# The planner's table of durations and landings revised in a list-scheduled two-layer mixer block

## The chip, the cores and the metric

The kernel runs on one core of a Trainium2 chip. The metric is device time of one execution in microseconds (us), the median of several runs of the same program. One further execution is recorded by the hardware profiler; its rows are what is read below.

## What is computed

The reference is a block of two layers (`DEPTH = 2`) for 256 latent tokens and 256 context tokens of width 1024, all in float32. Cut to what matters:

```python
for l in range(DEPTH):
    need_ctx = l < DEPTH - 1
    hl = xl * (1.0 + sc1) + sh1                      # sc, sh, g: from w_ada[l] and the conditioning vector
    hc = xc * (1.0 + xsc1) + xsh1
    out_l, out_c = token_mixers(hl, hc, ...)         # one input projection, 4 mixers, gated sum, out projection
    xl = layer_norm(ALPHA * xl + g1 * out_l, ...)
    hl = xl * (1.0 + sc2) + sh2
    xl = layer_norm(ALPHA * xl + g2 * swiglu(hl, w_gate_up[l], w_down[l]), ...)
    if need_ctx:
        ...                                          # the same for the context tokens
return xl
```

The four mixers are multi-head latent attention (MLA), neighbourhood attention, differential attention and grouped-query attention (GQA). Each one's output goes through a projection of its own, is multiplied by a sigmoid gate, and the four are summed. In the second layer the context tokens are only keys and values, so its later parts work on 256 columns where the first layer's work on 512.

## The kernel before, in words

**Tiles.** Tokens lie along the free dimension: `hh` and `hl` hold the modulated input of all 512 tokens, eight tiles of 128 channels. A float32 product is made of three passes on TensorE (`mm3`): every operand `x` is split into a rounded part `hi` and a rest `lo`, and hi·hi, hi·lo and lo·hi are accumulated. A weight of 128 x 1024 (512 KB) is loaded by SyncE's queue into `wr`, ScalarE casts it to `wh`, VectorE subtracts to get `wl`; each of the three has a ring of three buffers (`load_w`). So a weight is a chain load, cast, subtract, and then its matmuls `mm<-wh,hh`, `mm<-wl,hh`, `mm<-wh,hl`.

**Stages.** For each layer: adaLN vectors (in the first layer by strips of 32 columns, `st<-wr,cc`, later by VectorE reductions `raw<-wr,silbc`), input projection, the four mixers, gates (`gt`), branch products (`mm<-y,wh`, `mm<-y,wl`), out projection, layer norm, the FFN with 22 tiles of 128, layer norm. Some steps move data between partitions by DMA from SBUF to SBUF (`q<-raw`, `k<-q`, `l<-q`, `k<-k`). GpSimd does the small powers: `rk`, `rq`, `rms`, `rg`, `lnr` to the exponent -0.5 (`mhalf`).

**What sets the order.** The program is not written in the order in which it runs. All operations are first recorded in a `Plan` (11034 of them); `price` gives each a cost in us, and `schedule` makes ten list schedules (`PASSES = 10`). `forward` simulates the five engines, the rotating buffers, and one DMA queue, and at each step takes the ready operation of the highest priority on the engine that can start first. `backward` simulates from the end and sets the priorities for the next pass. The forward order of the smallest modelled length is kept, and `emit` writes each engine's operations in it, one phase after the other. Nothing of the model runs on the chip: there each engine takes its instructions in the order written and waits on semaphores. All instructions therefore carry the line number of the emitting line (L540; strips L538), and the rows are told apart by tile names.

The names that matter: `Op`'s slots (L205), `price` (L281), `backward` (L331; DMA at L367 to L370), `forward` (L381; DMA at L479 to L483).

Of the kernel before, what the change touches and what calls it, by code (L numbers as in the profile page):

```python
# [11 lines left out]
F32R = mybir.dt.float32r  # L12
# [191 lines left out]

class Op:  # L205
    __slots__ = ("eng", "meth", "args", "kw", "phase", "idx", "preds", "succs", "npred", "tiles", "cost",
                 "prio", "prio2", "rest", "nafter", "start", "end", "est", "nrot", "bytes", "dge", "ins", "lab")


class _Eng:  # L210
# [21 lines left out]
class Plan:  # L232
# [47 lines left out]
    def price(self, op, ins, outs):  # L280

        eng, kw = op.eng, op.kw
        if eng == "tensor":
            if op.meth == "matmuls":
                return sum(k["rhs"].free() for k in kw["each"]) / 2400 / 4 * (1 if kw["each"][0]["rhs"].dtype == F32R else 4) + 0.1
            if op.meth == "transpose":
                n = kw["in_"].shape[0]
                return max(64, n) * 2.1 / 2400
            n = max(64, kw["rhs"].free())
            return n / 2400 + 0.0026 if kw["rhs"].dtype == F32R else n * 4 / 2400 + 0.43  # L290
        n = max([v.free() for v in outs + ins] or [1])
        ps_in = any(v.tile.pool.psum for v in ins)
        ps = ps_in or any(v.tile.pool.psum for v in outs)
        if eng == "scalar":
            ptr = sum(1 for k in ("bias", "scale") if isinstance(kw.get(k), View)) + ("accum_out" in kw)
            return (0.05 if ps_in else 0.09) + n * 0.833e-3 + 0.093 * ptr
        if eng == "vector":
            if op.meth == "reciprocal":
                return 0.065 + n * 8 / 960
            ptr = sum(1 for k in ("scalar", "scalar1", "scalar2") if isinstance(kw.get(k), View))  # L300
            if op.meth == "tensor_scalar" or op.meth == "tensor_copy":
                return 0.065 + 0.06 * ptr + n / 960 / (1 if ps else 2)
            return 0.065 + 0.065 * ptr + n / 960
        if eng == "gpsimd":
            if kw.get("op") == ALU.pow:
                return 0.3 + n * 0.17
            return 0.16 + n * 2.2e-3
        op_bytes = 1
        for v in (outs or ins):
            op_bytes = v.shape[0] * v.free() * 4  # L310
        op.bytes = op_bytes
        op.dge = 0.65 if outs and ins else 0.46
        return 0.05

    def schedule(self):
# [19 lines left out]
    def backward(self, order):  # L335

        ready = {e: [] for e in self.ENGINES}
        free = {e: 0.0 for e in self.ENGINES}
        heirs = {}
        for op in order:  # L340
            after = set(op.succs)
            for t in op.tiles:
                if t.next is not None:
                    after |= t.next.users
            op.nafter, op.rest = len(after), 0.0
            heirs[op] = after
        before = {op: [] for op in order}
        for op in order:
            for s in heirs[op]:
                before[s].append(op)  # L350
            if op.nafter == 0:
                ready[op.eng].append(op)
            for t in op.tiles:
                t.turn = 0.0
        dma, done = 0.0, 0
        while done < len(order):
            best = None
            for e in self.ENGINES:
                if ready[e]:
                    t = max(free[e], min(o.rest for o in ready[e]))  # L360
                    if best is None or t < best[0]:
                        best = t, e
            t, e = best
            op = max((o for o in ready[e] if o.rest <= t + LOOK_BACK), key=lambda o: (o.end, o.idx))
            ready[e].remove(op)
            t = max(t, op.rest)
            if e == "sync":  # L367
                dma = max(dma, t + 0.95) + max(op.bytes / 360e3, op.dge)
                free[e] = dma - 0.95
                op.prio2 = dma + 1.1  # L370
            else:
                free[e] = op.prio2 = t + op.cost
            done += 1
            for p in before[op]:
                p.rest = max(p.rest, op.prio2 + SEE[p.eng].get(e, SEE_OTHER[p.eng]))
                p.nafter -= 1
                if p.nafter == 0:
                    ready[p.eng].append(p)
        for op in order:
            op.prio = -op.prio2  # L380
            for t in op.tiles:  # L381
                t.turn = min(t.turn, op.prio)

    def forward(self):
# [13 lines left out]
        def grant(tile, slot):  # L398
            if slot.last is not None:
                slot.last.next = tile  # L400
            tile.slot, slot.last = slot, tile
            for w in tile.waiters:
                w.est = max(w.est, slot.ready)
                w.nrot -= 1
                if w.npred == 0 and w.nrot == 0:
                    push(w)

        queue, slots, first = {}, [], []
        for ph, pools in enumerate(self.phases):
            at, new = 0, []  # L410
            for p in pools:
                for tag, row in p.tags.items():
                    size = -(-max(t.row for t in row) * 4 // 32) * 32
                    row = sorted((t for t in row if t.left), key=lambda t: t.turn)
                    n = min(len(row), row[0].bufs if row else 0)
# [17 lines left out]
        free = {e: 0.0 for e in self.ENGINES}  # L433
# [8 lines left out]
        def advance(e):  # L442
            while cur[e] < nph and nleft.get((e, cur[e]), 0) == 0:
                cur[e] += 1
                for o in held[e].pop(cur[e], []):
                    ready[e].append(o)

        def push(op):
            if op.phase > cur[op.eng]:
                held[op.eng].setdefault(op.phase, []).append(op)  # L450
            else:
                ready[op.eng].append(op)
# [8 lines left out]
        dge_free, dma_free, done, order = 0.0, 0.0, 0, []  # L461
        while done < len(ops):
            best = None
            for e in self.ENGINES:
                if not ready[e]:
                    continue
                t = max(free[e], min(o.est for o in ready[e]))
                if best is None or t < best[0]:
                    best = (t, e)
            if best is None:  # L470
                return None
            t, e = best
            lim = t + LOOK[e]
            op = min((o for o in ready[e] if o.est <= lim), key=lambda o: (o.prio, o.idx))
            ready[e].remove(op)
            op.start = max(t, op.est)
            free[e] = op.start + op.cost
            op.end = free[e]
            if e == "sync":  # L479
                dge_free = max(op.end, dge_free) + op.dge  # L480
                dma_free = max(dge_free + 0.65, dma_free) + op.bytes / 360e3
                op.end = dma_free + 0.95
                free[e] = max(free[e], dma_free - 2.5)  # L483
            see = op.end + SEE_OTHER[e]
            order.append(op)
            done += 1
            nleft[(e, op.phase)] -= 1
            for s in op.succs:
                s.est = max(s.est, op.end + SEE[e].get(s.eng, SEE_OTHER[e]))
                s.npred -= 1  # L490
                if s.npred == 0 and s.nrot == 0:
                    push(s)
            for tl in op.tiles:
                if tl.pool.psum:

                    for o in tl.users:
                        if o.eng != e:
                            o.est = max(o.est, op.end + SEE[e].get(o.eng, SEE_OTHER[e]))
                tl.left -= 1
                slot = tl.slot  # L500
                slot.ready = max(slot.ready, see)
                if tl.left == 0:
                    q = queue[(tl.pool, tl.tag)]
                    if q:
                        grant(q.pop(), slot)
                        continue
                    for new, t in slot.after:
                        new.ready = max(new.ready, slot.ready)
                        new.wait -= 1
                        if new.wait == 0:  # L510
                            grant(t, new)
            advance(e)
# [1312 lines left out]
```

## Time and profile before

| | us |
|---|---|
| median of 3 runs | 1368.88 |
| lowest, highest | 1368.81, 1370.12 |
| profiled execution | 1369.86 |
| its span, first to last instruction | 1367.9 |
| TensorE busy | 1347.7 |
| VectorE busy | 989.7 |
| ScalarE busy | 643.1 |
| GpSimd busy | 65.4 |

The profiled execution lies 0.98 us above the median, and 1.96 us of it lie outside the span. A matmul's busy time overlaps with the next one's, and its end is modelled, so TensorE's busy share says only that it rarely stood idle. How often it did is in the rows of its waits, and in the starts of neighbouring rows of its timeline: in a timeline row the first number is the start, the second the length of the row, and a bracket names the idle time ahead of it and what ended that. The mean granted clock of TensorE is 0.998 of full speed.

### The profile page before, as it was taken

What the parts mean: (1) busy time and instruction counts of PE and PEld (TensorE: products, weight loads), DVE (VectorE), ACT (ScalarE), POOL (GpSimd) and SP (SyncE); (2) the same over time, 40 slices, a digit from 0 to 9 for tenths busy, and PEclk for the clock granted to TensorE, in tenths of its full rate; (3) what the DMA queues carried; (4) which work ended last, traced back from release to release, by engine and by line L of the source; (5) the groups of instructions that cost most, each with busy time, mean ns of one, the idle gap of its engine ahead of it and who ended that gap; (6) DMA issues with size and microseconds to landing.
All of it is one profiled execution on the core that took longest, in us unless ns stands there. A gap on an engine that the chain in (4) does not pass through costs nothing.

```text
span 1367.9 us, 20685 instructions
## 1 busy us (share of the span) xinstructions
PE 1347.7 (99%) x7804; PEld 1171.5 (86%) x7804; DVE 989.7 (72%) x1753; ACT 643.1 (47%) x1160; POOL 65.4 (5%) x124
## 2 busy tenths in 40 slices
PE   7999999999999999999999999999999999999997
PEld 4789889888878889888888888899999899899986
DVE  3697899997875778777655463868979878855554
ACT  3576676633754422223222121467857566544430
POOL 0000100122000000000000000101000200000000
PEclk9999999999999999999999999999999999999999
DMA  8843534355246615556666754355344367565550
GB/s 305 290 131 103 162 103 120 103 161 155 80 151 201 209 45 160 174 185 198 216 190 198 216 183 133 104 161 161 106 135 148 125 209 270 192 186 181 186 180 31
DMA packets 72819, 223.83 MB, mean 164 GB/s; under 512 B 9696, under 2 KB 13968, under 8 KB 72720
## 3 DMA queue, kind: packets, MB, share of 16 engines
q1 hardware_dynamic: 72720, 222.52, 51.1%
q8 instruction: 61, 1.00, 0.3%
q14 instruction: 38, 0.31, 0.1%
HBM read 212.76 MB, written 1.07 MB: 156 GB/s over the span
## 4 chain that ended last, share of the span: by engine, by line
PE 92%; DVE 2%; DMA 2%; ACT 1%; POOL 1%; issue 1%; SPq 0%; POOLq 0%; DVEq 0%; ACTq 0%
PE mm L540 81%; PE st L540 7%; PE o L540 3%; DMA wr<-in_w_out 1%; PE st L538 1%; DVE wl L540 1%; DMA wr<-in_w_ada 1%; ACT wh L540 0%; DMA wr<-in_w_ckv 0%; POOL rms L540 0%; DVE x L540 0%; POOL rk L540 0%; DMA wr<-in_w_br 0%; DMA q<-raw 0%; DVE raw L540 0%
## 5 line engine op out<-in xcount | busy, mean ns | idle before, releaser
L540 ACT CAST wh<-wr 128x1024 fp32r<-128x1024 f32 (+2 forms) x261 | 265.8, 1024 | 388.4 <-PE mm L540 310.8
L540 PE MATMUL mm<-hh,wh 128*128 128x512 f32 (+1 forms) x1248 | 424.0, 341 | 1.4 <-ACT wh L540 1.0
L540 PE MATMUL mm<-hl,wh 128*128 128x512 f32 (+1 forms) x1246 | 423.1, 340 | 0.0
L540 PE MATMUL mm<-hh,wl 128*128 128x512 f32 (+1 forms) x1248 | 422.7, 340 | 0.0
L540 DVE TENSOR_TENSOR wl<-wr,wh 128x1024 fp32r<-128x1024 f32 (+3 forms) x260 | 308.9, 1192 | 151.5 <-ACT wh L540 147.7
L540 PEld LDWEIGHTS mm<-hh,wh 128*128 128x128 f32 x1248 | 235.9, 189 | 27.5 <-ACT wh L540 2.0
L540 PEld LDWEIGHTS mm<-hh,wl 128*128 128x128 f32 x1248 | 235.5, 189 | 24.6 <-issue 0.4
L540 PEld LDWEIGHTS mm<-hl,wh 128*128 128x128 f32 x1246 | 236.0, 189 | 23.4 <-DVE hl L540 0.3
L540 DVE CUSTOM_DVE_ANT_0 y<-wr,silbc 128x1024 bf16<-128x1024 f32 x80 | 96.6, 1223 | 42.4 <-DMA wr<-in_w_ada 42.4
L540 PE MATMUL mm<-wl,hh 128*128 128x256 f32 (+3 forms) x344 | 110.5, 322 | 0.0
L540 PE MATMUL mm<-wh,hh 128*128 128x256 f32 (+3 forms) x344 | 110.4, 323 | 0.0
L540 PE MATMUL mm<-wh,hl 128*128 128x256 f32 (+3 forms) x344 | 110.2, 321 | 0.0
L540 PE MATMUL mm<-wl,fh 128*128 128x512 f32 (+1 forms) x270 | 102.1, 378 | 0.0
L540 PE MATMUL mm<-wh,fh 128*128 128x512 f32 (+1 forms) x270 | 101.3, 376 | 0.0
L540 PE MATMUL mm<-wh,fl 128*128 128x512 f32 (+1 forms) x270 | 101.1, 375 | 0.0
L540 DVE TENSOR_REDUCE s<-st 128x1 f32<-128x512 f32 (+1 forms) x120 | 70.7, 598 | 8.7 <-PE st L540 6.8
L540 ACT ACTIVATE P<-st,s 128x512 f32<-128x512 f32 (+1 forms) x96 | 59.1, 617 | 28.7 <-DVE s L540 27.7
L540 PEld LDWEIGHTS mm<-wh,hh 128*128 128x128 f32 x344 | 64.8, 189 | 4.9 <-DVE y L540 0.5
L540 PE MATMUL mm<-y,wh 128*128 128x512 f32 (+1 forms) x256 | 68.7, 344 | 0.2 <-ACT wh L540 0.2
L540 PEld LDWEIGHTS mm<-wh,hl 128*128 128x128 f32 x344 | 65.0, 189 | 3.9
L540 PEld LDWEIGHTS mm<-wl,hh 128*128 128x128 f32 x344 | 65.0, 189 | 3.8
L540 DVE TENSOR_TENSOR ptl<-st,pth 128x512 fp32r<-128x512 f32 (+1 forms) x96 | 56.7, 596 | 8.0 <-ACT pth L540 7.1
(267 smaller groups left out, 1956.4 us busy)
## 6 DMA issues: line engine op xcount, KB each, us to landing
wr<-in_w_ada SPq DMA_DIRECT2D x87, 512.0 KB, 3.7
wr<-in_w_gu SPq DMA_DIRECT2D x80, 512.0 KB, 4.4
wr<-in_wa SPq DMA_DIRECT2D x74, 512.0 KB, 3.9
wr<-in_w_dn SPq DMA_DIRECT2D x44, 512.0 KB, 3.3
wr<-in_w_br SPq DMA_DIRECT2D x16, 512.0 KB, 3.5
wr<-in_w_out SPq DMA_DIRECT2D x16, 512.0 KB, 5.1
wr<-in_w_gq SPq DMA_DIRECT2D x8, 512.0 KB, 3.4
bc<-in_lnrows SPq DMA_DIRECT2D x16, 256.0 KB, 3.3
```

The source lines that it names most:

```text
L538: o.ins = nc.tensor.matmul(**{k: real(v) for k, v in m.items()})
L540: o.ins = getattr(getattr(nc, o.eng), o.meth)(*args, **kw)
```

## The change

Only the planner's numbers change. No operation, tile, buffer or shape is added or taken away; both kernels record the same 11034 operations.

```diff
     __slots__ = ("eng", "meth", "args", "kw", "phase", "idx", "preds", "succs", "npred", "tiles", "cost",
-                 "prio", "prio2", "rest", "nafter", "start", "end", "est", "nrot", "bytes", "dge", "ins", "lab")
+                 "prio", "prio2", "rest", "nafter", "start", "end", "est", "nrot", "bytes", "dge", "late", "ins", "lab")
...
         if eng == "tensor":
             if op.meth == "matmuls":
-                return sum(k["rhs"].free() for k in kw["each"]) / 2400 / 4 * (1 if kw["each"][0]["rhs"].dtype == F32R else 4) + 0.1
+                return sum(k["rhs"].free() for k in kw["each"]) / 2400 + 0.1
             if op.meth == "transpose":
-                n = kw["in_"].shape[0]
-                return max(64, n) * 2.1 / 2400
-            n = max(64, kw["rhs"].free())
-            return n / 2400 + 0.0026 if kw["rhs"].dtype == F32R else n * 4 / 2400 + 0.43
+                return 0.108 if kw["in_"].shape[0] > 32 else 0.09
+            n = max(256, kw["rhs"].free())
+            return n / 2400 + (0.0134 if n < 512 else 0.0156)
...
         if eng == "gpsimd":
             if kw.get("op") == ALU.pow:
-                return 0.3 + n * 0.17
-            return 0.16 + n * 2.2e-3
+                return 0.4 + n * 0.17
+            return 0.3 + n * 0.6e-3
...
-        op.dge = 0.65 if outs and ins else 0.46
+        op.dge, op.late = (0.65, 1.5) if outs and ins else (0.46, 0.4)
         return 0.05
...
             if e == "sync":
-                dma = max(dma, t + 0.95) + max(op.bytes / 360e3, op.dge)
-                free[e] = dma - 0.95
+                dma = max(dma, t + 0.95 + op.late) + max(op.bytes / 340e3, op.dge)
+                free[e] = dma - 0.95 - op.late
                 op.prio2 = dma + 1.1
...
             if e == "sync":
                 dge_free = max(op.end, dge_free) + op.dge
-                dma_free = max(dge_free + 0.65, dma_free) + op.bytes / 360e3
-                op.end = dma_free + 0.95
+                dma_free = max(dge_free + 0.65, dma_free) + op.bytes / 340e3
+                op.end = dma_free + 0.95 + op.late
                 free[e] = max(free[e], dma_free - 2.5)
```

In numbers of the model: a matmul of 512 columns goes from 0.2159 to 0.2289 us, one of 256 from 0.1093 to 0.1201, a transpose of 128 rows from 0.112 to 0.108; a small GpSimd operation on a few columns from 0.16 to 0.30, a power on four columns from 0.98 to 1.08; a 512 KB load's transfer from 1.46 to 1.54 and its landing 0.4 later; a move from SBUF to SBUF lands 1.5 later.

Every engine's order changes in many places, by a few rows each. Three places on TensorE are shown.

TensorE in the first layer, MLA: the last matmuls of the gate block (`mm<-hh,wh` and its two partners, 512 columns) that stand between the products of the compressed key-value projection and the transposes of its normed rows (`raw`). Before:

```order
L540 MATMUL mm_1738<-hl_84,wh_1639 128x512
L540 MATMUL mm_1738<-hh_83,wl_1650 128x512
L540 MATMUL mm_1738<-hh_83,wh_1639 128x512
L540 MATMUL mm_1782<-ident_60,raw_1694 128x128
L540 MATMUL mm_1782<-ident_60,raw_1711 128x128
L540 MATMUL mm_1782<-ident_60,raw_1746 128x128
L540 MATMUL mm_1782<-ident_60,raw_1754 128x128
```

And now:

```order
L539 MATMUL mm_1720<-hh_83,wh_1627 128x512
L539 MATMUL mm_1720<-hl_84,wh_1627 128x512
L539 MATMUL mm_1774<-ident_60,raw_1688 128x128
L539 MATMUL mm_1774<-ident_60,raw_1725 128x128
L539 MATMUL mm_1774<-ident_60,raw_1739 128x128
L539 MATMUL mm_1774<-ident_60,raw_1746 128x128
```

The gate matmuls between the last key-value product and the first transpose are 16 before (the 667th to the 682nd row of TensorE's order) and 20 now (667th to 686th): four more stand ahead of the transposes.

TensorE in the second layer, GQA: `qr` are the normed and rotated queries and keys, transposed by TensorE; `st<-k,q` are the first scores, whose `q` comes by the move `q<-raw`; between them are matmuls of 256 columns. Before, the end of the transposes and, further on, the first scores:

```order
L540 MATMUL mm_10952<-ident_60,qr_10876 128x128
L540 MATMUL mm_10957<-ident_60,qr_10851 128x128
L540 MATMUL mm_10957<-ident_60,qr_10876 128x128
L540 MATMUL mm_10965<-hh_83,wh_10839 128x256
L540 MATMUL mm_10965<-hl_84,wh_10839 128x256
L540 MATMUL mm_10965<-hh_83,wl_10942 128x256
```

And now:

```order
L539 MATMUL mm_10952<-y_3_10746,wh_10758 128x256
L539 MATMUL mm_10952<-y_2_10753,wh_10758 128x256
L539 MATMUL mm_10952<-y_3_10746,wl_10769 128x256
L539 MATMUL mm_10963<-ident_60,qr_10817 128x128
L539 MATMUL mm_10963<-ident_60,qr_10869 128x128
L539 MATMUL mm_10976<-hh_83,wh_10843 128x256
```

Six branch products now stand between the transposes, ahead of the last two; and from the last transpose to the first score `st<-k,q` there are 35 matmuls before (the 5316th to the 5350th row) and 43 now (5318th to 5360th).

TensorE in the first layer, where the out projection begins: the branch products (`mm<-y,wh`, `mm<-y,wl`) between the last gate matmul, `mm<-hh,wl`, and the first transpose of an adaLN column, `st<-ident,ada`. Behind that transpose come, in both orders, eight matmuls of the following weights, one more small transpose and then the first matmul with a `wl` that VectorE has to finish. Before:

```order
L540 MATMUL mm_4637<-y_4_3600,wh_4297 128x512
L540 MATMUL mm_4675<-y_5_3586,wh_4297 128x512
L540 MATMUL mm_4675<-y_4_3600,wh_4297 128x512
L540 MATMUL mm_4637<-y_5_3586,wl_4318 128x512
L540 MATMUL mm_4637<-y_3_3701,wh_4297 128x512
L540 MATMUL mm_4637<-y_0_3713,wh_4297 128x512
L540 MATMUL mm_4637<-y_3_3701,wl_4318 128x512
L540 MATMUL mm_4675<-y_5_3586,wl_4318 128x512
L540 MATMUL mm_4675<-y_3_3701,wh_4297 128x512
L540 MATMUL mm_4675<-y_0_3713,wh_4297 128x512
L540 MATMUL mm_4675<-y_3_3701,wl_4318 128x512
L540 MATMUL st_4718<-ident_60,ada_0_66 8x128
```

And now:

```order
L539 MATMUL mm_4649<-hh_83,wl_4546 128x512
L539 MATMUL mm_4671<-y_4_3613,wh_4272 128x512
L539 MATMUL mm_4640<-y_1_3706,wh_4272 128x512
L539 MATMUL mm_4640<-y_0_3714,wh_4272 128x512
L539 MATMUL mm_4640<-y_1_3706,wl_4301 128x512
L539 MATMUL mm_4671<-y_5_3606,wl_4301 128x512
L539 MATMUL mm_4671<-y_1_3706,wh_4272 128x512
L539 MATMUL mm_4671<-y_0_3714,wh_4272 128x512
L539 MATMUL mm_4671<-y_1_3706,wl_4301 128x512
L539 MATMUL st_4718<-ident_60,ada_0_66 8x128
```

Eleven branch products stand there before (the 1820th to the 1830th row of TensorE's order) and eight now (1831st to 1838th).

## Rows read from the trace of the kernel before

**Rows 1.** The page: engines, and the shares of the chain that ended last.
```profile
PE 1347.7 (99%) x7804; PEld 1171.5 (86%) x7804; DVE 989.7 (72%) x1753; ACT 643.1 (47%) x1160; POOL 65.4 (5%) x124
...
PE 92%; DVE 2%; DMA 2%; ACT 1%; POOL 1%; issue 1%; SPq 0%; POOLq 0%; DVEq 0%; ACTq 0%
```

**Rows 2.** Windows: stretch, its length, busy us of each engine, clock, DMA share, GB/s.
```profile
core 0: us, PE busy (x) PEld busy (x) DVE busy (x) ACT busy (x) POOL busy (x), PEclk, DMA share, GB/s
0.00:16.00 16.00, 8.44 (x44) 3.56 (x45) 2.75 (x7) 4.89 (x9) 3.07 (x12) 1.00 0.88 320
...
140.00:160.00 20.00, 19.36 (x123) 17.29 (x122) 16.76 (x39) 12.84 (x28) 4.96 (x8) 1.00 0.52 155
160.00:280.00 120.00, 120.00 (x690) 103.53 (x689) 114.08 (x261) 80.47 (x193) 6.03 (x13) 1.00 0.37 112
280.00:300.00 20.00, 19.76 (x95) 15.99 (x94) 18.88 (x32) 6.35 (x10) 6.80 (x10) 1.00 0.57 176
300.00:395.00 95.00, 94.90 (x475) 79.02 (x474) 81.52 (x174) 51.41 (x102) 7.11 (x12) 1.00 0.43 137
395.00:435.00 40.00, 38.06 (x167) 30.68 (x166) 23.57 (x32) 18.16 (x22) 0.00 (x0) 1.00 0.53 171
435.00:512.00 77.00, 77.00 (x375) 64.01 (x374) 54.70 (x80) 24.49 (x38) 3.61 (x8) 1.00 0.40 131
512.00:740.00 228.00, 228.00 (x1075) 191.73 (x1074) 160.31 (x240) 65.77 (x88) 0.00 (x0) 1.00 0.60 188
...
860.00:960.00 100.00, 99.85 (x694) 94.03 (x693) 77.23 (x142) 63.54 (x122) 12.04 (x22) 1.00 0.47 148
...
1050.00:1125.00 75.00, 73.43 (x544) 68.38 (x543) 63.37 (x130) 48.25 (x94) 10.34 (x18) 1.00 0.49 163
```

**Rows 3.** TensorE's waits over the span: total us, times, longest.
```profile
PE st L538 <- DMA wr<-in_w_ada: 6.7, 2, 5.0
PE mm L540 <- DVE wl L540: 1.4, 1, 1.4
PE mm L540 <- ACT wh L540: 1.2, 3, 0.5
PE mm L540 <- ACT raw L540: 0.6, 1, 0.6
...
PE st L540 <- DMA q<-raw: 0.5, 1, 0.5
```

**Rows 4.** Timeline of TensorE, 148.9 to 150.6 us.
```profile
148.97 0.39 PE L540 MATMUL mm<-hh,wl 128*128 128x512 f32 x1
149.20 0.39 PE L540 MATMUL mm<-hh,wh 128*128 128x512 f32 x1
149.43 0.49 PE L540 MATMUL mm<-ident,raw 128*128 128x128 f32 x3
150.56 0.33 PE L540 MATMUL mm<-ident,raw 128*128 128x128 f32 x1 [0.64 <-ACT raw L540]
```

**Rows 5.** Timeline of TensorE, 1082.8 to 1084.3 us, and what stood behind its wait.
```profile
1083.34 0.28 PE L540 MATMUL mm<-hh,wh 128*128 128x256 f32 x1
1083.46 0.28 PE L540 MATMUL mm<-hl,wh 128*128 128x256 f32 x1
1084.21 0.47 PE L540 MATMUL st<-k,q 128*128 128x512 f32 x1 [0.47 <-DMA q<-raw]
...
1080.47 3.61 DMA q<-raw
```

**Rows 6.** Timeline of TensorE, 288.6 to 290.8 us, and GpSimd's part of the chain.
```profile
290.39 0.44 PE L540 MATMUL mm<-ident,qr 128*128 128x128 f32 x2 [0.24 <-DVE qr L540]
...
287.98 1.91 POOL rms L540
```

**Rows 7.** Timelines of TensorE and VectorE, 397 to 405 us.
```profile
397.50 0.39 PE L540 MATMUL mm<-hh,wl 128*128 128x512 f32 x1
...
402.19 0.27 PE L540 MATMUL st<-ident,ada 128*8 128x128 f32 x1
403.86 0.50 PE L540 MATMUL mm<-y,wl 128*128 128x512 f32 x1 [1.41 <-DVE wl L540]
...
399.58 0.69 DVE L540 SCALAR_TENSOR_TENSOR gt<-gt,mm 128x512 f32<-128x512 f32 x1 [0.28 <-PE mm L540]
```

**Rows 8.** VectorE's split of a weight, by form: count, busy us, mean ns.
```profile
L540 DVE TENSOR_TENSOR wl<-wr,wh 128x1024 fp32r<-128x1024 f32 x238 | 289.8, 1222 | 140.1 <-ACT wh L540 136.3 <-DMA wr<-in_w_gu 0.2
```

**Rows 9.** Moves between partitions, from issue to landing: count, KB each, median us.
```profile
k<-k SPq DMA_DIRECT2D x12, 128.0 KB, 2.9
k<-q SPq DMA_DIRECT2D x24, 64.0 KB, 2.0
```

## The prediction

> **What bounds the kernel now.** I read the page first. TensorE is busy for 99% of the span and carries 92% of the chain that ended last [rows 1]. That alone does not say that there is nothing to win, since matmuls overlap and their ends are modelled. So I took the windows next, cut where the stages change [rows 2]: TensorE's clock is 1.00 in each, so no stretch is slow by its clock. TensorE is without a gap in 435 to 740 us (77.00 of 77.00 and 228.00 of 228.00), the out projection and the FFN, and has idle time in only a few others: 7.56 us before 16 us, where the first weights are still on their way, then 0.64 in 140 to 160, 0.24 in 280 to 300, 0.10 in 300 to 395, 1.94 in 395 to 435, 0.15 in 860 to 960 and 1.57 in 1050 to 1125. These six add up to 4.64 us. The list of TensorE's waits puts names to them [rows 3]: one for a `wl` (1.4), three for a `wh` (1.2), one for `raw` (0.6), one for a move `q<-raw` (0.5). The 6.7 us for `w_ada` are the start.
>
> A wait costs a little more than its idle time, because the matmul ahead of it ends after the next could have begun: rows of 512 columns start 0.23 us apart but last 0.39 [rows 4], rows of 256 start 0.12 apart and last 0.28 [rows 5], so 0.16 goes missing per wait. With some ten such waits, the most that a better order can give back after the start is an estimated 4.64 + 10 x 0.16 = 6.2 us, 0.45% of the time.
>
> **The change, part by part.** No instruction is added or removed, so TensorE's work stays: what can move is only where a wait falls. Transposes are split into a few more runs; a run interrupts the stream of matmuls for no time that I could see, so I cost that at nothing, covered by TensorE's own pipeline; if it were not, three more runs at 0.1 us would be 0.3.
>
> *The matmul prices.* The new prices, 0.229 us for 512 columns and 0.120 for 256, are the spacings of the rows, 0.23 [rows 4] and 0.12 [rows 5]; the old 0.216 and 0.109 were short by 6 and 9%. A planner that thinks TensorE faster than it is feeds it too early, not too late. The cost of that is buffers taken early, and TensorE's full windows show none. Direct gain 0.
>
> *MLA's normed rows in the first layer.* TensorE reaches the fourth transpose at 149.7 us and waits until 150.56, 0.64 of idle time for ScalarE's `raw`, which waits for GpSimd's `rk` [rows 4]. Four more matmuls of 512 columns now stand ahead, 4 x 0.23 = 0.92 us. The wait is worth 0.64 + 0.16 = 0.8, so the cover is enough if GpSimd's chain starts no later. Late next is the split of these transposes, with a little less cover behind it. Bounds -0.8 and 0; I take -0.8.
>
> *GQA's scores in the second layer.* TensorE waits 0.47 us for the landing of `q<-raw`, which took 3.61 us [rows 5], so 0.63 in all. Cover from the last transpose to the score grows from 35 to 43 matmuls, 8 x 0.12 = 0.96 us, but those six branch products ahead of the last two transposes also make these later where `q` hangs on them. Bounds -0.63 and +0.3; I take -0.6.
>
> *Differential attention's norm.* TensorE waits 0.24 + 0.16 = 0.4 us for `qr`, which waits for GpSimd's `rms`, 1.91 us long [rows 6]. Between the transposes of the `y` before it and the last `qr` there are 26 matmuls of 512 columns before and 24 now: 2 x 0.23 = 0.46 us of cover lost. Bounds 0 (GpSimd's chain may end as much earlier) and +0.5; I take +0.4.
>
> *The first layer's out projection.* TensorE reaches the first `wl` at about 402.3 us and starts it at 403.86 [rows 7]: this is the kernel's longest wait after the start. Of the branch products behind the last gate, eleven become eight, so 3 x 0.23 = 0.69 us of cover goes. VectorE's work behind the gate (two `y`, two `gt`, two `x`, the `wl`) is the same, but it stood idle 0.28 us for a branch product there [rows 7], which now comes earlier. So +0.69 - 0.28 = +0.4; bounds -0.1 and +0.7.
>
> *GpSimd's prices, the loads' 0.4 us and the rate.* They act only through the places above. SyncE's list of FFN loads keeps its shape, and the FFN is full: 0. In the second layer the start of the out projection, most of the 1.57 us in 1050 to 1125 [rows 2], has its twelve branch products in both orders: 0, with the wait gone or doubled as bounds, ±0.8.
>
> *The start.* SyncE's first thirteen loads keep their order; after that one `xT` comes ahead of one `w_ada`. The DMA engines are 88% busy there [rows 2], so an exchange of two loads, 256 KB at 320 GB/s or 0.8 us, is the bound: ±0.8, taken as 0.
>
> The sum: -0.8 - 0.6 + 0.4 + 0.4 = -0.6 us. Against the profiled execution, 1369.86, that is 1369.3. This execution lies 0.98 above the median of the runs, so on the median's scale I forecast 1368.3, from 1368.88. With all bounds at one end the sum is -0.8 - 0.6 + 0 - 0.1 - 0.8 - 0.8 = -3.1, at the other 0 + 0.3 + 0.5 + 0.7 + 0.8 + 0.8 + 0.3 = +3.4; they will not all fall together, so the forecast's own range is 1366.2 to 1370.7, about 2.2 us either way.
>
> **A price that the trace disputes.** The new model lets a 64 KB move land 0.65 + 0.65 + 64/340 (0.19) + 0.95 + 1.5 = 3.94 us after issue, the old one 2.44. The `q<-raw` above took 3.61 [rows 5], but the 24 moves `k<-q` of 64 KB took 2.0 in the median and the twelve `k<-k` of 128 KB 2.9 [rows 9]. So the old price was right for most moves and the new one for the one that TensorE waited for; the rest are now priced up to 1.9 us too late. The Trainium skill, "DMA: Bandwidth & Descriptors", section "Anatomy of one DMA", gives about 2.0 us fixed plus the bytes at 436 GB/s, measured on the GpSimd path; for 64 KB that would be an estimated 2.15 us. By that rule, the trace of `k<-q` agrees and this part of the change is an error; it is the ground of the second rival.
>
> **The rivals.**
>
> *Faster: the truer model closes most gaps.* The planner optimises the length of its own model, and one that knows where TensorE really stands can place the last matmuls ahead of each wait. At its best all 6.2 us go: 1362.7. With the two large places kept as I read them in the order (1.94 and 1.57), a good half is left to win, 3.3 us, for 1365.6. For it: the trace confirms the matmul prices, and GpSimd's chains stand behind two of the waits. Against it: at the longest wait the cover shrinks, and the other large one keeps its cover. I give it 0.26.
>
> *Slower: VectorE in 160 to 280 us.* The mis-priced moves `k<-q` and `l<-q` lie there. In the backward pass a landing 1.5 us later gives everything that feeds a move a higher priority by that much, so splits of heads go ahead of splits of weights on VectorE, which is busy for 114.08 of 120.00 us there [rows 2] and so has 5.9 us of slack in all. Each `wl` split that is pushed behind comes 1.22 us later [rows 8] for a weight whose matmuls follow at once. It decides from three such splits on, 3 x 1.22 = 3.7 us, giving 1368.3 + 3.7 = 1372.0; all the slack used twice over in both layers would be more. For it: rows 9 against the price. Against it: TensorE has no gap in this stretch now, and it has matmuls of other branches to fill with. I give it 0.17.
>
> *The change does nothing.* The list schedules could settle on an order whose waits are the old ones with other names: 1368.9. The three places above did move, so only 0.07.
>
> **How the numbers follow.** My forecast has 0.50, the faster rival 0.26, the slower 0.17, no effect 0.07. About 0.2%, or 2.7 us, is what a measurement of this kernel can tell from no change: faster is below 1366.1, slower above 1371.6. Nearly all of the forecast and of no effect lies between these; of the forecast I leave 0.02 on each side; the faster rival counts as faster but for 0.02 of it, the slower one wholly but for 0.01. So faster 0.26, same 0.56, slower 0.18. The range reaches from 1363.5, which leaves out only the faster rival's extreme, to 1372.5, just past the slower one's price.
>
> **What would show it.** In the profile after, the wait for ACT `raw` at about 150 us and that for `q<-raw` at about 1083 us should be gone; the wait for `wl` at about 402 us should be there still and longer, some 1.8 us of idle time; 435 to 740 us should stay full. The windows' idle time from 16 to 1340 us should be 4 us, not 4.6. I am wrong if TensorE's idle time there falls below 2 us or the wait at 402 us is gone (the faster rival), if TensorE waits for `wl` in 160 to 280 us (the slower one), or if the start of the strips moves by over a microsecond.

## The result, and the profile after

The changed kernel takes 1380.45 us (median of 4 runs, 1378.33 to 1380.56) against 1368.86: a ratio of 1.0079 with a 95% interval of 1.0061 to 1.0096. It is slower by 0.8%, 11.6 us, outside the range of the prediction and on the side to which it gave 0.18.

The page of the changed kernel, engines and chain, to be read against [rows 1]:

```profile
PE 1353.1 (98%) x7804; PEld 1171.4 (85%) x7804; DVE 984.8 (71%) x1753; ACT 642.5 (47%) x1160; POOL 69.7 (5%) x124
...
PE 81%; DVE 10%; ACT 3%; DMA 2%; POOL 2%; issue 2%; SPq 0%; POOLq 0%; DVEq 0%; ACTq 0%
```

No engine has more instructions. What changed is the chain: TensorE carried 92% of it and now 81%, VectorE 2% and now 10%. TensorE is still the bound, but it is handed its inputs late more often. Its waits, against [rows 3] (total us, times, longest; the 6.7 us for `w_ada` at the start are as before):

```profile
PE mm L539 <- DVE qr L539: 2.2, 4, 0.9
PE mm L539 <- DVE wl L539: 1.3, 2, 1.0
PE mm L539 <- ACT raw L539: 1.0, 2, 0.8
PE o L539 <- ACT pth L539: 0.9, 1, 0.9
PE mm L539 <- DVE gt L539: 0.8, 2, 0.5
...
PE st L539 <- DVE x L539: 0.5, 1, 0.5
...
PE mm L539 <- DVE hh L539: 0.4, 1, 0.4
PE st L539 <- ACT P L539: 0.3, 1, 0.3
PE st L539 <- DVE y L539: 0.3, 1, 0.3
PE st L539 <- DMA q<-raw: 0.3, 1, 0.3
```

No wait is long. They have become many, on `qr`, `pth`, `gt`, `x`, `hh`, `P`: the ends of quite different chains. The windows tell where, against [rows 2]:

```profile
140.00:160.00 20.00, 19.20 (x128) 17.59 (x127) 14.09 (x33) 12.12 (x27) 6.22 (x8) 1.00 0.49 156
160.00:280.00 120.00, 119.66 (x678) 102.24 (x676) 115.67 (x261) 79.12 (x190) 2.46 (x7) 1.00 0.38 117
280.00:300.00 20.00, 18.58 (x94) 14.47 (x93) 17.88 (x36) 8.03 (x17) 10.96 (x16) 1.00 0.31 104
...
435.00:512.00 77.00, 77.00 (x352) 62.88 (x352) 55.00 (x78) 23.22 (x33) 2.55 (x6) 1.00 0.42 139
512.00:740.00 228.00, 228.00 (x1096) 192.49 (x1095) 158.35 (x241) 67.11 (x92) 1.05 (x2) 1.00 0.57 184
...
860.00:960.00 100.00, 99.06 (x666) 92.14 (x665) 77.50 (x136) 58.61 (x109) 8.46 (x16) 1.00 0.44 136
```

435 to 740 us is full as before, as the prediction said; the mixer stages, 140 to 300 and from 860 on, have more idle time in nearly every window. From 16 to 1340 us TensorE is idle for 9.7 us, where 4.6 stood before and 4 were predicted. The signs named for the two rivals did not come either.

Idle time does not count the whole, since a row's modelled end hides the first part of a wait. So I also added up, over all 7804 matmul starts of the trace, by how much each step from one start to the next is longer than the usual step of its kind (0.228 us for 512 columns, 0.120 for 256, 0.109 for a transpose). This **lateness** is 26.0 us before and 36.7 after. The difference of 10.7 is that of the spans (1367.9 and 1378.6), as it must be with the same matmuls on both sides, and 0.9 less than that of the medians, because the profiled execution before lay 1 us above its median. What the sum tells is where the time went. After the first 46 us, 13 steps before are late by over 0.2 us, 7.0 us together; after the change 24 are, 13.6 us together. The growth by stage: 1.0 us in the first 46, 1.0 to 160, 3.3 to 300, none from 300 to 880, 1.1 to 960, 1.2 to 1050, 2.0 to 1135, 1.2 to 1200.

### The profile page after: what moved, and what is told of

Its sections match the earlier page's. It is cut to its first block, busy times and chain, and to the rows that moved or that the text cites. A ratio compares the mean times of both kernels' runs of the same rounds, so it can differ in the third digit from the quotient of the medians.

```text
span 1378.6 us, 20686 instructions
## 1 busy us (share of the span) xinstructions
PE 1353.1 (98%) x7804; PEld 1171.4 (85%) x7804; DVE 984.8 (71%) x1753; ACT 642.5 (47%) x1160; POOL 69.7 (5%) x124
## 4 chain that ended last, share of the span: by engine, by line
PE 81%; DVE 10%; ACT 3%; DMA 2%; POOL 2%; issue 2%; SPq 0%; POOLq 0%; DVEq 0%; ACTq 0%
PE mm L539 72%; PE st L539 6%; PE o L539 3%; DVE wl L539 2%; DVE s L539 2%; ACT P L539 1%; DVE raw L539 1%; POOL rms L539 1%; DVE P L539 1%; DMA wr<-in_w_out 1%; DVE ptl L539 1%; DVE x L539 1%; ACT wh L539 1%; PE st L537 1%; DVE y L539 1%
## 5 line engine op out<-in xcount | busy, mean ns | idle before, releaser
L539 DVE CUSTOM_DVE_ANT_0 raw<-wr,silbc 128x1024 bf16<-128x1024 f32 x48 | 58.1, 1216 | 4.1 <-DMA wr<-in_w_ada 4.0
```

What stands on the lines that cost most here:

```text
L539: o.ins = getattr(getattr(nc, o.eng), o.meth)(*args, **kw)
```

## The experiments

The theories: **A**, TensorE's old prices were short by 6 to 9% and so left a margin (time between the end of a result and its use) for every chain of other engines; **B**, the moves, now priced up to 1.9 us too late; **C**, the list schedule scatters with any change of a number. In all the experiments only the planner differs, never an operation. Ratios are against runs of the kernel before on the same chip (medians 1368.9 to 1369.9).

The last column shows theory A's margin in the traces. The planner stands in the kernel, so its order and its dependences can be laid beside a trace row by row. For every TensorE operation I took the last of its inputs that came from another engine or a move, and for every such result (some 880 between 46 and 1335 us) the time from its end to its first use. **Close** counts those used within 0.3 us.

| run | median us | ratio, 95% interval | close |
|---|---|---|---|
| before | 1368.86 | 1 | 27 |
| the change | 1380.45 | 1.0079, 1.0061 to 1.0096 | 82 |
| e1 TensorE's prices alone | 1390.03 | 1.0153, 1.0136 to 1.0170 | 93 |
| e2 landings alone | 1372.58 | 1.0026, 1.0016 to 1.0036 | 29 |
| e3 GpSimd's prices alone | 1375.82 | 1.0043, 1.0028 to 1.0058 | 33 |
| e4 the change without TensorE's | 1370.98 | 1.0011, 1.0002 to 1.0021 | 25 |
| e5 half of TensorE's | 1379.83 | 1.0071, 1.0050 to 1.0092 | 66 |
| e6 TensorE's the other way | 1376.93 | 1.0052, 1.0037 to 1.0067 | 30 |
| e7 the change, margin 0.5 us | 1372.56 | 1.0022, 1.0013 to 1.0031 | 33 |
| e8 the change, longer powers | 1377.06 | 1.0052, 1.0037 to 1.0067 | 67 |
| e9 before, nudged | 1372.64 | 1.0031, 1.0021 to 1.0041 | 27 |
| e10 before, nudged otherwise | 1370.06 | 1.0006, 0.9997 to 1.0016 | 33 |
| e11 the change, nudged | 1376.29 | 1.0055, 1.0038 to 1.0071 | 96 |
| e12 e1 with margin 0.5 us | 1386.72 | 1.0135, 1.0112 to 1.0157 | 33 |
| e13 e1, all else 8% up | 1373.75 | 1.0032, 1.0021 to 1.0044 | 37 |
| e14 e1 in forward only | 1389.92 | 1.0148, 1.0133 to 1.0163 | 57 |
| e15 e1 in backward only | 1379.38 | 1.0072, 1.0052 to 1.0092 | 37 |
| e16 e1, nudged | 1391.80 | 1.0157, 1.0141 to 1.0173 | 90 |
| e17 the change, other engines 8% up | 1371.70 | 1.0014, 1.0006 to 1.0023 | 24 |
| e18 e17 with longer powers | 1375.36 | 1.0039, 1.0026 to 1.0052 | 31 |

### Which part carries the loss: e1 to e4

e1 is the kernel before with the change's lines for `tensor` and nothing else; e2 with its lines for the DMA (`late`, 340e3); e3 with its lines for `gpsimd`; e4 is the change with the old `tensor` lines.

> Theory A (margin): the old TensorE prices, 6 to 9% short, made the planner put more matmuls between a chain and its consumer than it believed necessary; the new ones take that margin away. Then this part alone carries the loss: 1376 to 1382 us. Theory B (moves): the landings priced up to 1.9 us late carry it, and this part alone stays within 2 us of 1368.9. Theory C (scatter): any change of a price reshuffles the order and moves the time by some us either way, whatever the price is: anywhere in 1365 to 1382.

> Theory A: within 2 us of 1368.9. Theory B: 1376 to 1382 us, with the waits of the changed kernel. Theory C: anywhere in 1365 to 1382.

> Theories A and B: within 2 us of 1368.9, or a little below it, since two of the waits before were on GpSimd's powers. Theory C: anywhere in 1365 to 1382.

> The changed kernel with TensorE's old prices. Theory A: back to 1367 to 1371 us. Theory B: still 1376 to 1382. Theory C: anywhere in 1365 to 1382, and not the sum of what the two parts give alone.

TensorE's prices alone cost 1.5%, twice the loss of the whole change and more than any theory had allowed (A to 1382, C to 1382); without them the change is 0.1% from the kernel before. B falls: the landings alone are 0.26% slower. e3 is a miss of A and B, which had it within 2 us: GpSimd's prices alone cost 6.5 us, 2.2 in one wait for `q<-raw`, and with the landings added (e4) the loss is 1.7. The parts do not add up (20.7 + 3.3 + 6.5 us alone, 11.6 together), as C has it. TensorE's waits in e1:

```profile
PE st L539 <- DMA q<-raw: 2.6, 2, 1.7
PE mm L539 <- DVE qr L539: 2.4, 3, 1.7
PE st L539 <- ACT P L539: 2.0, 2, 1.5
PE mm L539 <- DVE gt L539: 1.8, 2, 1.0
PE mm L539 <- ACT raw L539: 1.8, 3, 0.9
PE mm L539 <- ACT wh L539: 1.6, 3, 0.9
PE o L539 <- ACT pth L539: 1.3, 2, 1.1
```

The picture of the change, larger: chains through a move, ScalarE, VectorE and GpSimd are all late. 32 steps after 46 us are late by over 0.2 us, 23.3 us together. Nine of them are late by over 1 us and hold 12.3; the change has three such steps, 3.3 us, and the kernel before one, 1.6. The rest of e1's late steps is much as in the change. So e1 is the change's loss and, on top, a few long waits.

### How large is the scatter: e9 to e11 and e16

e9 nudges a VectorE price by 0.002 us, e10 a ScalarE price; e11 and e16 make e9's edit in the change and in e1.

```diff
-            return 0.065 + 0.065 * ptr + n / 960
+            return 0.065 + 0.067 * ptr + n / 960
```
```diff
-            return (0.05 if ps_in else 0.09) + n * 0.833e-3 + 0.093 * ptr
+            return (0.05 if ps_in else 0.09) + n * 0.833e-3 + 0.095 * ptr
```

> The kernel before with one VectorE price moved by 0.002 us per pointer operand, which means nothing on the chip but reorders the list. It measures the scatter of the list schedule itself. Theory A without much scatter: within 2 us of 1368.9. Theory C: some us away, up to the 8 us of the kernel with less TensorE price, and mostly above, if the kernel before was a lucky member.

> The same with one ScalarE price moved by 0.002 us per pointer operand. Theory A without much scatter: within 2 us of 1368.9. Theory C: some us away, and not by as much as the first.

> The changed kernel with the same VectorE price moved by 0.002 us. Theory A without much scatter: 1378 to 1382 us. Theory C: some us away from 1380.4; if it comes down to the nudged kernels of before, the change itself cost nothing beyond the scatter.

> TensorE's new prices alone with one VectorE price moved by 0.002 us per pointer operand. If the 21 us are the prices' own: 1385 to 1393 us. If 1390 is an outlier of the scatter: 1375 to 1383, where the changed kernel and its nudged neighbour lie.

A number that means nothing moves the time by 3.8, 1.2, 4.2 and 1.8 us. Four nudges show the size of the scatter and not its bound; e3 may be more of it. So differences of up to some 4 us between two of these kernels (e2, e4, e7 to before; e8 to the change; e18 to e17) can be a reshuffle, and of the change's own 11.6 us some 4 may be. TensorE's prices stand outside: 1390.0 and, nudged, 1391.8. The close results hardly move with a nudge: 27 and 33 for the kernel before with 27, 96 for the change with 82, 90 for e1 with 93.

### More and less of the price: e5 and e6

```diff
-            return n / 2400 + 0.0026 if kw["rhs"].dtype == F32R else n * 4 / 2400 + 0.43
+            return n / 2400 + (0.008 if n < 512 else 0.0091) if kw["rhs"].dtype == F32R else n * 4 / 2400 + 0.43
```
```diff
-            return n / 2400 + 0.0026 if kw["rhs"].dtype == F32R else n * 4 / 2400 + 0.43
+            return n / 2400 - (0.0082 if n < 512 else 0.0104) if kw["rhs"].dtype == F32R else n * 4 / 2400 + 0.43
```

> The kernel before with matmul prices half-way to the new ones (0.2224 us for 512 columns, 0.1147 for 256). Theory A (the old price's shortfall was a margin): between the two, 1372 to 1386 us. Theory C (scatter): anywhere in 1365 to 1390.

> The kernel before with matmul prices as far below the old ones as the new ones are above (0.2029 and 0.0985 us). Theory A: more margin, so no slower than before, 1364 to 1369 us, unless the planner then fetches so early that buffers run out. Theory C: anywhere in 1365 to 1390.

With 512 columns at 0.203, 0.216, 0.222 and 0.229 us the kernel takes 1376.9, 1368.9, 1379.8 and 1390.0 (the last, e1, has new prices for transposes and strips as well). Upward the loss grows as A has it. Downward A missed: more of the "margin" costs 8 us too, more than the nudges, and with only 30 close results. What costs these 8 us stays open. So it is no margin of which more is better; of these four prices the old one is the best, and a higher and a lower one both lose.

### A margin in us, and the powers: e7, e12, e8

e7 (on the change) and e12 (on e1) let TensorE see results 0.5 us later in the model:

```diff
-SEE = {"tensor": {"tensor": 0.0}, "scalar": {"scalar": 0.1, "tensor": 0.24, "gpsimd": 0.07},
-       "vector": {"vector": 0.128, "tensor": 0.23, "gpsimd": 0.156}, "gpsimd": {"gpsimd": 0.1, "vector": 0.07},
-       "sync": {}}
+SEE = {"tensor": {"tensor": 0.0}, "scalar": {"scalar": 0.1, "tensor": 0.74, "gpsimd": 0.07},
+       "vector": {"vector": 0.128, "tensor": 0.73, "gpsimd": 0.156}, "gpsimd": {"gpsimd": 0.1, "vector": 0.07},
+       "sync": {"tensor": 0.5}}
```

e8 gives GpSimd's powers in the change the length that rows show (1.9 us for four columns, [rows 6]):

```diff
-                return 0.4 + n * 0.17
+                return 0.57 + n * 0.33
```

> The changed kernel with its true prices, and the margin written down as one: in the model TensorE sees results of ScalarE, VectorE and the moves 0.5 us later than it does. Theory A: the loss goes, 1364 to 1371 us. If the TensorE prices hurt in another way than by lost margin, it stays near 1380.

> The kernel with TensorE's new prices alone (1390.0 us) plus the written margin of 0.5 us. Theory A: most of the 21 us loss goes, 1368 to 1375 us. Theory C: it falls to somewhere in 1369 to 1385 like any reshuffle.

> The changed kernel with GpSimd's powers priced by the rows (0.57 + 0.33 n: 0.90 us for one column, 1.89 for four) in place of 0.57 and 1.08. Theory A: the waits for raw and qr behind GpSimd's rk, rms and rg go, some 4 us of the 11.6: 1375 to 1378 us. If it were the powers alone that the margin covered, the whole loss goes: 1367 to 1371.

e7 comes back to 1372.6, a little above A's range; e12 only to 1386.7, outside the ranges of both A and C. Both have 33 close results, so the written margin did restore the margin. In the change that was nearly enough. In e12 it was not: ten steps are late by over 1 us, 16.0 us together, and three stretches ran at a lower clock (last section). Long waits like those of e1 and e12 so have another cause, which no run here shows. In e8 the waits behind the powers shrink as expected:

```profile
PE mm L539 <- DVE qr L539: 0.5, 1, 0.5
PE mm L539 <- ACT raw L539: 0.4, 2, 0.2
```

`qr` had 2.2 and `raw` 1.0 in the change. The time falls by 3.4 us, as expected, but that is within the scatter; that the powers cause a part of the loss is likely, not shown.

### The ratio to the rest: e13, e17, e18

e13 is e1 with every other price up by 8%: the prices of the other engines as below, their latencies in `SEE` and `SEE_OTHER`, and the DMA queue's numbers (333e3 for 360e3, 0.70 for 0.65, 1.03 for 0.95 and so on). e17 is the change with the same for the engines and latencies, its DMA numbers left as they are; e18 adds e8's powers.

```diff
-SEE_OTHER = {"tensor": 0.2, "scalar": 0.132, "vector": 0.13, "gpsimd": 0.2, "sync": 0.0}
+SEE_OTHER = {"tensor": 0.216, "scalar": 0.143, "vector": 0.14, "gpsimd": 0.216, "sync": 0.0}
...
-        op.cost = self.price(op, ins, outs)
+        op.cost = self.price(op, ins, outs) * (1 if op.eng == "tensor" else 1.08)
```

> TensorE's new prices alone, and every other engine's prices, latencies and the DMA queue's numbers 8% up, which brings back the old ratio between TensorE and the rest (old to new is 6% for 512 columns and 10% for 256). Theory A as a matter of ratio: 1369 to 1375 us. If the new TensorE prices hurt for another reason than their ratio to the rest: 1384 to 1392.

> The changed kernel with the prices and latencies of ScalarE, VectorE and GpSimd 8% up (the DMA queue as changed). Theory A as a matter of ratio: 1369 to 1375 us, the loss gone but for the scatter. If the changed kernel's loss were another one than that of TensorE's prices alone: 1376 to 1382.

> The same with GpSimd's powers by the rows (0.57 + 0.33 n, before the 8%). If the powers' waits are the next largest of the rest: 1 to 4 us below the one before it, and so about the time of the kernel before, 1366 to 1371 us. If the 8% already cover them: no different from it by more than the scatter of 1 to 4 us.

e13 takes 16.3 us off e1, with TensorE's new prices in place; e17 brings the change itself to within 0.14% of the kernel before. Both are as expected. e13 is far beyond the scatter; e17 is 8.8 us below the change, but only 4.6 below its nudged neighbour e11 (5.6 when each is taken against the kernel before on its chip), barely more than a nudge. Its close results speak more clearly: 24, against 82 and 96. So TensorE's price does not hurt by itself, but by standing 6 to 10% higher against the others. With longer powers on top, e18 did not gain the 1 to 4 us that it should have if their waits were the next largest; it is 3.7 us slower than e17, no more than a reshuffle. No version beat the kernel before.

### Forward or backward: e14 and e15

`op.cost2`, priced with the other `tensor` lines, is used in `backward` alone: e14 has the new lines in `forward` and the old ones in `backward`, e15 the reverse.

```diff
         op.cost = self.price(op, ins, outs)
+        op.cost2 = self.price(op, ins, outs, True)
...
-                free[e] = op.prio2 = t + op.cost
+                free[e] = op.prio2 = t + op.cost2
```

> TensorE's new prices in the forward simulation only, the priorities set with the old ones. If the loss comes from forward, which takes a consumer as soon as the model calls it ready: 1383 to 1392 us, the same as 1390.0 within the scatter. If it comes from the priorities: 1369 to 1375.

> TensorE's new prices in the priorities only, the old ones in the forward simulation. If the loss comes from forward: 1369 to 1375 us. If from the priorities: 1383 to 1392.

New prices in `forward` alone give the whole loss of e1; in the priorities alone they give 10 us, half of it, where one or the other had been expected. Both act; the simulation forward, which decides what is ready when, acts more. The size for the priorities is rough: e15's four runs go from 1376.2 us at a mean granted clock of 0.998 to 1383.2 at 0.994, so some of its 10 us are clock (last section).

## Why the prediction was wrong

**The step that failed is the first of the sum**, the matmul prices, "Direct gain 0". The prices were read rightly: 0.23 and 0.12 us are what the change puts in. What followed was wrong: that a planner which thinks TensorE too fast pays for it only with buffers taken early, and that TensorE's full windows show a cost of nothing. The short price was worth something. `forward` puts a consumer where the model calls its input ready, and prices count only against each other. With each matmul priced 6 to 9% short, the matmuls that the planner put between a result and its use lasted longer than it believed, everywhere, also where nothing waited. This reserve took up what the model has wrong elsewhere, and the true price alone takes it away.

That the loss hangs on the ratio of TensorE's prices to the rest is shown by e1, e4 and e13. That the reserve shrinks is shown by the close results: 27 before, 82 in the change, 93 in e1, 66 with half of the price, and 25, 37 and 24 where the old price or the old ratio is back (e4, e13, e17). Each of the seven kernels with more than 50 of them loses over 7 us. The reverse does not hold: e6, e12 and e15 lose 8 to 18 us with 30 to 37. So the lost reserve accounts for the change, but for a scatter of some 4 us, and not for all of e1.

**What the reserve had covered** is shown in part. A power on four columns is priced at 1.08 us and takes 1.9 [rows 6]. The move `q<-raw` ahead of GQA's scores takes 5.28 us in the changed kernel (below), where even the new model says 3.9 for its 64 KB on an empty queue. VectorE is not a piece of it. Its chain in the changed kernel ahead of the first `wl` of the out projection:

```profile
406.67 0.68 DVE L539 SCALAR_TENSOR_TENSOR gt<-gt,mm 128x512 f32<-128x512 f32 x1
407.27 1.29 DVE L539 TENSOR_TENSOR x<-x,gt 128x512 f32<-128x512 f32 x2
408.47 3.49 DVE L539 TENSOR_TENSOR wl<-wr,wh 128x1024 fp32r<-128x1024 f32 x3
```

`gt`, two `x` and the first `wl` begin 0.60 us apart, without a gap, and the model prices `gt` and `x` at 0.598. Over the whole trace before, 936 VectorE instructions that were followed directly by another took 559 us from start to start, for a price of 551, and 512 of ScalarE 308 for 301: short by 1.4 and 2.1%, where TensorE's old price was short by 6 to 9. So the change brought the three engines' prices closer together, and the 8% of e13 and e17 does not correct the others but puts the reserve back in another place. Which of the errors counts most stays open: e8 and e18 priced the powers alone, and neither moved the time beyond the scatter; no run priced the moves by their rows.

**The places were too few.** I priced the four places at which the kernel before waits most clearly in the moved rows. With 0.16 us added to each idle time, they came out so:

- *MLA's normed rows*, -0.8 predicted. The four matmuls do stand ahead, and the wait is there still. The bound had a condition, "if GpSimd's chain starts no later", and that failed. TensorE's timeline and the chain, against [rows 4]:

```profile
151.71 0.52 PE L539 MATMUL mm<-ident,raw 128*128 128x128 f32 x3
153.03 0.33 PE L539 MATMUL mm<-ident,raw 128*128 128x128 f32 x1 [0.81 <-ACT raw L539]
```
```profile
149.70 2.78 POOL rk L539 x2
152.47 0.02 issue
152.50 0.48 ACT raw L539
```

  TensorE comes 2.3 us later than before (151.71 for 149.43), GpSimd's last `rk` pair ends 2.5 us later, at 152.47 for about 150.0. The wait grew from 0.80 to 0.97, outside the bounds of -0.8 and 0.
- *GQA's scores*, -0.6 predicted. The longer cover helped, but the move takes 5.28 us where it took 3.61 [rows 5]; it is now issued 0.9 us behind a load and 0.55 behind a `k<-k`, where it was 1.5 and 1.1:

```profile
1094.60 0.70 PE L539 MATMUL st<-k,q 128*128 128x512 f32 x2 [0.31 <-DMA q<-raw]
```
```profile
1089.18 5.28 DMA q<-raw
```

  The wait fell from 0.63 to 0.47, by 0.16, a quarter of the term.
- *Differential attention's norm*, +0.4 predicted. There are now two waits, and both behind `rms`, against [rows 6]:

```profile
295.00 0.44 PE L539 MATMUL mm<-ident,qr 128*128 128x128 f32 x2 [0.28 <-DVE qr L539]
...
297.48 0.44 PE L539 MATMUL mm<-ident,qr 128*128 128x128 f32 x2 [0.65 <-DVE qr L539]
```

  Together 1.25 for 0.4: +0.85, the right sign, twice the size and outside the bound of +0.5.
- *The first layer's out projection*, +0.4 predicted. Less cover, but VectorE's chain ended earlier by as much, against [rows 7]:

```profile
407.98 0.50 PE L539 MATMUL mm<-hh,wh 128*128 128x512 f32 x1
408.32 0.40 PE L539 MATMUL mm<-hl,wh 128*128 128x512 f32 x1
409.74 0.50 PE L539 MATMUL mm<-y,wl 128*128 128x512 f32 x1 [1.03 <-DVE wl L539]
```

  1.2 us ahead of the `wl` and 0.35 ahead of the `mm<-hh,wh` (407.98 after a small transpose at 407.61), 1.55 together for 1.57: 0.

In sum +0.8 for -0.6, so the four places missed by only 1.4 us. The other 9.9 of the 10.7 us of lateness arose where I had costed nothing: at the start (1.0, a term with bounds of ±0.8), and above all at chains that made no wait before. The 0.18 for the side on which the time fell came from the slower rival, whose mechanism did not appear; that it stood there was luck.

**The rivals.** The faster one, a truer model that closes gaps, had the wrong sign; its price of 3.3 us was also added up wrongly, since 6.2 without the two large places, 1.94 and 1.57, is 2.7. The slower one, VectorE in 160 to 280 us, had the sign but not the mechanism: there is no wait for a `wl` in that stretch and only 0.34 us of idle time. Its ground, the landings, costs 3.3 us alone (e2), of which scatter may be all. The sentence drawn from the Trainium skill ("DMA: Bandwidth & Descriptors", section "Anatomy of one DMA", an estimated 2.15 us for 64 KB) is near `k<-q`, with a median of 2.0 us before and 2.5 in the changed kernel, but not the move that TensorE waited on, 5.28. No run here took the landing prices out of the change alone.

## What to carry to other kernels

A price that is too short can be a reserve. Where a planner sets the order, making one engine's price true takes away what had covered the errors of the others, so look for those errors first, or write the reserve down in their place; here that brought the time back to within 0.3% (e7, e17), and more of the short price did not help (e6). Before a price change is called harmless because the bound engine is full, ask which chains are covered now and by how much; the waits of the profile list only those that already failed. And where a list schedule sets the order, nudge a meaningless number first: here that alone moved the time by up to 4 us, and no difference smaller than that says anything of a price.

## What the runs showed that I had not expected

After some waits of about 2 us the granted clock of TensorE fell. In e12 TensorE idled 1.99 us ahead of a `wh`, and then ran at its lower level, 1.2 GHz: windows (length, TensorE busy, clock, DMA share, GB/s) and timeline of e12:

```profile
430.00:438.00 8.00, 8.00 (x37) 1.00 0.64 203
...
440.00:444.00 4.00, 3.66 (x10) 0.61 0.54 182
444.00:447.00 3.00, 3.00 (x14) 0.95 0.89 281
```
```profile
440.34 0.50 PE L539 MATMUL mm<-hh,wh 128*128 128x512 f32 x1 [1.99 <-ACT wh L539]
...
442.62 0.63 PE L539 MATMUL mm<-hh,wl 128*128 128x512 f32 x1
443.05 0.63 PE L539 MATMUL mm<-hh,wh 128*128 128x512 f32 x1
...
444.56 0.39 PE L539 MATMUL mm<-hl,wh 128*128 128x512 f32 x1
444.79 0.39 PE L539 MATMUL mm<-hh,wl 128*128 128x512 f32 x1
```

From about 441 to 444 us a matmul of 512 columns took 0.43 us from start to start, then 0.23 again: some eight matmuls, 1.6 us on top of the wait. The same followed waits of about 2 us near 1092 and 1151 us in that run (clock 0.57 in 1096 to 1100 and 0.66 in 1153 to 1158 us). Its profiled execution so holds an estimated 4 us at the lower level (1.6, 1.7 and about 1 us, the lengths of the windows by what their clocks lack, less idle time), which clouds it as a test of the margin. Not every such wait did this: in the same run TensorE idled 2.02 us from 65 us on, and the clock of 64 to 74 us is 1.00. The profiled executions of e14, e15 and e17 hold one, two and one stretch of this kind (in e15, clock lowered from 1093.0 us on, after a wait of 1.79). The kernel before and the changed one have no stretch at the lower level between 16 us and the last 30.
